# Handing five kinds of buffers to the most urgent tile, with a trace to plan and a trace to build

## The chip, the cores and the metric

The kernel runs on one NeuronCore of a Trainium2 chip. A core has five engines that run side by side, each in its own program order: TensorE (PE in the profile; its weight loads are shown apart as PEld), VectorE (DVE), ScalarE (ACT), GpSimd (POOL) and SyncE (SP), which here issues nearly all DMA transfers. Engines wait for each other through semaphores. The metric is the device time of one execution in microseconds (us), as the median over runs.

## The reference

One inference step of a small decoder of two layers, for a prompt of 2048 tokens and for 8 sample tokens that share the weights and have 2048 cached positions each. All arithmetic is float32. Cut to what matters:

```python
for layer in range(2):
    if layer == 0:   # even: gated MLP (A) beside stick-breaking attention (B)
        u, v, gate_a, q, k, vb, gate_b = split(x @ w_in_even)
        out_a = chunk_spatial_gate(gelu(u), standardize(gelu(v))) * silu(gate_a)
        z = q @ k.T * HEAD_DIM ** -0.5
        att = exp(log_sigmoid(z) + later)      # later: reversed cumulative sum of log_sigmoid(-z)
        out_b = (att @ vb) * silu(gate_b)
    else:            # odd: attention over 256 selected keys (C) beside causal pooling (D)
        q, kv, q_idx, k_idx, w_idx, gate_c, p, gate_d = split(x @ w_in_odd)
        index = einsum(relu(q_idx @ k_idx.T), w_idx)
        sel = top_k(index, 256)
        out_c = softmax(q @ k[sel].T + bias) @ v[sel] * silu(gate_c)
        out_d = (windowed_means(p) - p) @ w_grp * scale * silu(gate_d)
    x = layer_norm(alpha * x + concat(outs) @ w_out[layer])
```

The outputs are the two activations and the new cache rows of both layers.

## The kernel before

**The work.** The prompt goes in four blocks of 512 tokens. `load_xT` transposes a block of x, `p0` (layer 0) and `p1a`, `p1b` (layer 1) project it, `mixer_b` is the attention B, `select` and `topk` find the 256 keys, `c_tiles` is the attention C, `out_proj` the output projection, `ln_late` and `ln` the layer norm. The sample tokens go along in `sample0` and `sample1`. Projections are three float32r matmuls for each float32 one: high part by high part, low by high, high by low (`pp` at L735 to L737, `pp_o` at L1132 to L1134); ScalarE casts the high part of a weight (L661) and VectorE subtracts the low part (L664).

`run` weaves these generators into one traced program. In B, a tile `z` of logits comes from TensorE (L1027), ScalarE reads it out (L1031 or L1034), VectorE scans it (L1041), TensorE transposes the result (`ps_p`, L1064), ScalarE copies it back (L1065), and `av` sums it up (L1073). In C, `z_c` (L1763) is read out by VectorE together with its maximum (L1765), ScalarE takes the exponential (L1781), TensorE transposes (`ps_pc`, L1794), ScalarE copies back (L1796), and `av_c` sums (L1808). The indexer's scores are `z_i` (L1453), read by ScalarE (L1456). At the end of each `topk` VectorE runs a conditional (L1595) that goes into an exact search only if there are ties.

**The buffers.** A tile comes from a pool under a tag, and tiles of one tag share a number of buffers. In PSUM each of the tags `pp`, `pt` and `pz` has two buffers of one bank (2 KB a partition). `BANKS` says which tile uses which: `pp` takes pp, pp_o, ps_ki, ps_kv; `pz` takes z, z_c, z_i, ps_s, ps_m; `pt` takes ps_p, ps_pc, ps_x and every other name that is not listed. In SBUF the tags `tmp` and `ot` have four buffers each; `tmp` holds short-lived pieces, among them lng and lnb, the gains and offsets of the layer norm (L1210, L1211), and `ot` holds loaded pieces (xc, the transposed block's input, and ot, the input of `out_proj`).

**What sets the order.** After the trace the class `Order` replans it. `gather` collects the dependencies, the tiles' users (`uses`) and for each tag the tiles in traced order (`tags`). `plan` is a list scheduler: it steps through time with costs by `cost` (a conditional counts 400 ns) and picks on each engine the ready instruction of smallest `rank`; ranks come from `latest`, which runs the plan backwards. An instruction is ready when its predecessors are done and its tiles have buffers. `settle` makes plans for three guesses of the costs, with five rounds each, and keeps the one that `replay` finds shortest under two draws of the costs. `keep` hands each engine's order to the framework, which makes the semaphores and assigns buffers.

In `plan`, `take` hands out buffers: for each tag strictly in traced order, and only when the tile that got the last one has begun (`open_`):

```python
while queue[g] and free[g] and open_[g]:
    x = queue[g].pop()
    if gone[g]:
        self.after[x] = gone[g].pop(0)
    free[g] -= 1
    open_[g] = False
```

`after` notes which tile left the buffer that x gets.

Of the kernel before, what the change touches and what calls it, by code (L numbers as in the profile page):

```python
# [11 lines left out]
F32 = mybir.dt.float32  # L12
# [10 lines left out]
P = 128  # L23
# [59 lines left out]
}  # L83


class Order:


    ENGINES = {"PE": "PE", "DVE": "DVE", "Activation": "ACT", "Pool": "POOL", "SP": "SP"}
    SEM, DMA_START, DMA_END, RATE = 200, 700, 1500, 280.0  # L90
    TILED, STAY, PATIENT = 150, 500, 40e3
    GUESSES = ((1.0, 200), (1.0, 250), (1.04, 230))
    ROUNDS, DRAWS, SPREAD = 5, 2, 0.05
    TAIL = {"ACT": 100, "POOL": 45, "DVE": 75}
# [47 lines left out]
    def gather(self):  # L142
# [83 lines left out]
        for t in sorted(self.uses, key=lambda t: self.uses[t][0]):  # L226
            if self.tiles[t].space != DRAM:
                self.tags.setdefault(self.tiles[t].tag, []).append(t)


    def cost(self, n):
# [83 lines left out]
        return (i.opcode in ("TensorScalarPtr", "TensorCopy") and len(i.outs) == 1 and self.size(i.outs[0]) > 1  # L315
                and all(map(sb, (*full, i.outs[0]))))

    def settle(self):

        N, eng = len(self.ins), self.eng  # L320
        self.costs = [self.cost(n) for n in range(N)]
        for g, ms in self.group.items():
            busy = sum(self.costs[m][0] for m in ms)
            self.costs[g] = busy, busy + 170
        self.dma = [e is not None and "DMA" in i.opcode for e, i in zip(eng, self.ins)]
        self.kinds = [self.kind(n) for n in range(N)]
        self.ports = [self.port(n) for n in range(N)]
        self.succ = [[] for _ in range(N)]
        for n, d in enumerate(self.dep):
            for m in d:  # L330
                self.succ[m].append(n)
        self.links()
        draws, mid, best = [self.draw(k) for k in range(self.DRAWS)], self.costs, None
        sem = self.SEM
        for by, near in self.GUESSES:
            self.costs = [(b * by, l * by) if e in self.TAIL else (b, l) for e, (b, l) in zip(eng, mid)]
            self.SEM = near
            self.plan(list(range(N)))
            for _ in range(self.ROUNDS):
                self.SEM = near  # L340
                self.plan(self.latest())
                self.SEM = sem
                x = sum(self.replay(c) for c in draws)
                if best is None or x < best[0]:
                    best = x, self.order, self.after
        self.costs, (_, self.order, self.after) = mid, best

    def draw(self, seed):

# [75 lines left out]
    def turns(self):  # L425
# [11 lines left out]
            last[e] = n  # L437
        return out

    def plan(self, rank):  # L440

        N, eng, push, pop = len(self.ins), self.eng, heapq.heappush, heapq.heappop
# [2 lines left out]
        for g, ts in self.tags.items():  # L445
            for t in ts:
                home[t] = g
                for n in self.uses[t]:
                    left[n] += 1 + (n != self.uses[t][0])
                    tiles[n].append(t)  # L450
        queue = {g: ts[::-1] for g, ts in self.tags.items()}
        free = {g: max(self.tiles[t].tag_meta.bufs for t in ts) for g, ts in self.tags.items()}
        open_ = dict.fromkeys(queue, True)
        users = {t: len(u) for t, u in self.uses.items()}
        self.after, gone = {}, {g: [] for g in queue}
        since, done, self.begun = [0.0] * N, [0.0] * N, [0.0] * N
        ready, idle = {e: [] for e in self.ENGINES.values()}, dict.fromkeys(self.ENGINES.values(), 0.0)
        self.order = {e: [] for e in ready}
# [7 lines left out]
                push(due, (since[n], n))  # L466

        def take(g, t):
            while queue[g] and free[g] and open_[g]:
                x = queue[g].pop()  # L470
                if gone[g]:
                    self.after[x] = gone[g].pop(0)
                free[g] -= 1
                open_[g] = False
                for n in self.uses[x]:
                    release(n, t)

# [5 lines left out]
        while count < N:  # L483
            while back and back[0][0] <= now:
                _, g, x = pop(back)
                free[g] += 1
                gone[g].append(x)
                take(g, now)
            while due and due[0][0] <= now:
                n = pop(due)[1]  # L490
# [7 lines left out]
            for e, q in ready.items():  # L498
                while q and idle[e] <= now:
                    n, until = q[0][1], hold.get(self.OTHER.get(e), 0.0)  # L500
                    if e == "PE" and (kinds[n] == "h") != (kind == "h"):
                        same = [x for x in q if (kinds[x[1]] == "h") == (kind == "h") and x[0] <= q[0][0] + self.STAY]
                        if same:
                            n = min(same)[1]
                            q.remove(min(same))
                            heapq.heapify(q)
                            push(q, (-math.inf, n))
                    if e == "SP" and self.dma[n] and dma_end > now + self.DMA_START and last + rank[n] > now + self.PATIENT:
                        late.append(dma_end - self.DMA_START)
                        break  # L510
                    if ports[n] and until > now:
                        free_ = [x for x in q if not ports[x[1]] and now + cost[x[1]][0] <= until + self.SLACK]
                        if not free_:
                            late.append(until)
                            break
                        n = min(free_)
                        q.remove(n)
                        heapq.heapify(q)
                        n = n[1]
                    else:  # L520
                        pop(q)
                    s, (busy, lat) = now, cost[n]
                    if ports[n]:
                        hold[e] = s + max(40, busy - self.RELEASE[e])
                    if e == "PE" and now > idle[e] + 1 and kinds[n] == kind:
                        busy, lat = busy + self.RESTART, lat + self.RESTART
                    if e == "PE" and kinds[n] != kind:
                        s += self.TILED if "h" in (kinds[n], kind) else 0
                        kind = kinds[n]
                    self.begun[n] = s  # L530
                    if self.dma[n]:
                        dma_end = max(s + self.DMA_START, dma_end) + lat
                        done[n] = dma_end + self.DMA_END
                    else:
                        done[n] = s + lat
                    idle[e] = s + busy
                    self.order[e] += [*self.before.get(n, ()), *self.group.get(n, (n,))]
                    count += 1
                    moved = True
                    for m in succ[n]:  # L540
                        release(m, s + 1 if e == "PE" and eng[m] == "PE" else done[n] + self.SEM)
                    for t in tiles[n]:
                        g, u = home[t], self.uses[t]
                        if n == u[0]:
                            open_[g] = True
                            for m in u[1:]:
                                release(m, s)
                            take(g, s)
                        users[t] -= 1
                        if not users[t]:  # L550
                            push(back, (max(done[m] for m in u) + self.SEM, g, t))
# [59 lines left out]
                now = max([now] + [min(then)] if then else [now])  # L611
        return [-s - c[0] for s, c in zip(start, cost)]

    def keep(self):
        info = mybir.DependencyInfo(mybir.DependencyClass.NoSync, mybir.DependencyReason.DATA)
        for o in self.order.values():
            for a, b in zip(o, o[1:]):
# [5 lines left out]


class Body:
    def __init__(self, ctx, tc, I, O):
        self.ctx, self.tc, self.nc, self.I, self.O = ctx, tc, tc.nc, I, O
        pool = lambda n, b, **k: ctx.enter_context(tc.tile_pool(name=n, bufs=b, **k))
        self.cst = pool("cst", 1)
        self.sm = pool("sm", 4)  # L630
        self.dr = pool("dr", 1, space=DRAM)
        self.banks = {n: pool(n, 2, space=PSUM) for n in ("pp", "pt", "pz")}
        self.act = pool("act", 8)
        self.wp = pool("wp", 2)
        self.loc = pool("loc", 4)
        self.bufs = BUFS
# [30 lines left out]
    def rsqrt(self, out, var, eps, n):  # L667
# [9 lines left out]
        for _ in range(3):  # L677
# [2 lines left out]
            v.tensor_scalar(t[:n], t[:n], -0.5, 1.5, op0=OP.mult, op1=OP.add)  # L680
            v.tensor_tensor(out, out, t[:n], op=OP.mult)

    def ps(self, name, shape=(P, TB)):

        b = next(b for b in BANKS.get(name, "pt").split() if b in self.banks)
        return self.banks[b].tile(list(shape), F32, tag=b, name=name)

    def tmp(self, name):
        return self.loc.tile([P, TB], F32, tag="tmp", name=name, bufs=self.bufs["tmp"])

    def tok(self, name, n=TB):
        return self.loc.tile([P, TB + 16], F32, tag="tok", name=name, bufs=self.bufs["tok"])[:, :n]
# [392 lines left out]
            nc.sync.dma_start(self.otd[0][i][4 + m], sm)  # L1085

    def otile(self, name):
        return self.loc.tile([P, TB], F32, tag="ot", name=name, bufs=self.bufs["ot"])

    def out_parts(self, i, layer, last):  # L1090

# [1370 lines left out]
         ('new_d_buf_prompt', (1, 1, 15, 512)), ('new_d_buf_sample', (1, 8, 15, 512))]  # L2462


def build(nc, shapes):
    I = {n: nc.dram_tensor(n, s, d, kind="ExternalInput").ap() for n, s, d in shapes}
    O = {n: nc.dram_tensor("out_" + n, s, F32, kind="ExternalOutput").ap() for n, s in _OUTS}
    with tile.TileContext(nc, schedule_with_timeline_sim=True) as tc:
        with ExitStack() as ctx:
            body = Body(ctx, tc, I, O)  # L2470
            body.run()
        order = Order(tc, body.lags)
        order.gather()
        order.settle()
        order.keep()


# [11 lines left out]
```

## Time and profile before

| | |
|---|---|
| median of 3 runs | 2790.44 us (2785.44 to 2792.58) |
| the profiled execution | 2784.49 us |
| its span, first to last instruction | 2782.8 us |
| instructions | 52464 |
| HBM read and written | 431.33 MB and 89.73 MB, 187 GB/s over the span |

The page cuts the span into 40 slices; a digit is the busy share of a slice in tenths. TensorE's and VectorE's rows and the granted TensorE clock:

```profile
PE   9999999999999999989899999999999999899996
DVE  3466568775857886747988888897898788888865
PEclk9999999999999999999999999999999999999998
```

A busy TensorE is not one at its peak, because matmuls overlap and their ends are modelled. In the lists of waits each row says which instruction waited (engine, tile written, line), what came last before it could go, how many us in total, how often, and the longest.

### The profile page before, as it was taken

To read this page: it belongs to the slowest core of one execution; us is meant where nothing else is said; L and a number is where in the kernel's file an instruction comes from. 1 tells how busy PE (TensorE), PEld (TensorE's weight loads), DVE (VectorE), ACT (ScalarE), POOL (GpSimd) and SP (SyncE) were. 2 spreads that over 40 slices of the span, in tenths; PEclk is the share of its full clock that TensorE was granted. 3 is DMA by queue.
4 is the path that set the end of the run, shared out by engine and by line. 5 is a ranking of instruction groups with operands and counts; after the bars stand their busy time and mean duration, and the time that the engine had idled before them with its cause. 6 is when DMAs were issued, how large, how long until landed. Compare 5 with 4: busy or idle time off the path is not lost. (4 is left out here: it accounts for less than half of the span.)

```text
span 2782.8 us, 52464 instructions
## 1 busy us (share of the span) xinstructions
PE 2672.8 (96%) x17490; PEld 2154.5 (77%) x17490; DVE 2060.9 (74%) x5557; ACT 1604.3 (58%) x3216; POOL 766.3 (28%) x1040
## 2 busy tenths in 40 slices
PE   9999999999999999989899999999999999899996
PEld 7888787777777887768677677778777889898985
DVE  3466568775857886747988888897898788888865
ACT  3434333444444354435657677786686788688854
POOL 0111112210202321033433522334411445344222
PEclk9999999999999999999999999999999999999998
DMA  8666857895777777563764545433675666767462
GB/s 251 168 186 207 266 169 245 242 302 161 224 213 205 222 207 249 181 178 116 211 199 132 166 131 157 127 102 115 190 220 149 199 192 200 221 200 235 125 197 81
DMA packets 538914, 524.58 MB, mean 189 GB/s; under 512 B 43447, under 2 KB 411224, under 8 KB 538607
## 3 DMA queue, kind: packets, MB, share of 16 engines
q1 hardware_dynamic: 528759, 485.34, 58.9%
q0 software_dynamic: 9856, 35.66, 4.1%
q8 instruction: 139, 2.28, 0.3%
q14 instruction: 160, 1.31, 0.1%
HBM read 431.33 MB, written 89.73 MB: 187 GB/s over the span
## 5 line engine op out<-in xcount | busy, mean ns | idle before, releaser
L735 PE MATMUL pp<-xh,wh 128*128 128x512 f32 (+1 forms) x1536 | 624.0, 408 | 2.5 <-ACT wh L661 1.6
L736 PE MATMUL pp<-xl,wh 128*128 128x512 f32 (+1 forms) x1536 | 615.4, 401 | 0.0
L737 PE MATMUL pp<-xh,wl 128*128 128x512 f32 (+1 forms) x1536 | 613.6, 400 | 0.0
L664 DVE TENSOR_TENSOR wl<-wr,wh 128x512 fp32r<-128x512 f32 x520 | 354.5, 699 | 161.7 <-ACT wh L661 146.8
L661 ACT CAST wh<-wr 128x1024 fp32r<-128x1024 f32 x260 | 270.2, 1040 | 321.4 <-PE pp L736 160.2
L735 PEld LDWEIGHTS pp<-xh,wh 128*128 128x128 f32 (+1 forms) x1536 | 287.6, 188 | 67.4 <-issue 8.5
L737 PEld LDWEIGHTS pp<-xh,wl 128*128 128x128 f32 (+1 forms) x1536 | 287.6, 187 | 61.5 <-issue 4.4
L736 PEld LDWEIGHTS pp<-xl,wh 128*128 128x128 f32 (+1 forms) x1536 | 288.2, 188 | 53.9 <-issue 5.3
L1132 PE MATMUL pp_o<-wh,oh 128*128 128x256 f32 x1008 | 294.2, 294 | 5.4 <-DVE xres L1137 3.6
L1133 PE MATMUL pp_o<-wl,oh 128*128 128x256 f32 x1008 | 290.5, 289 | 0.2 <-DVE wl L664 0.2
L1134 PE MATMUL pp_o<-wh,ol 128*128 128x256 f32 x1008 | 288.5, 289 | 0.0
L1065 ACT COPY P<-ps_p 128x512 f32<-128x512 f32 (+2 forms) x320 | 166.5, 524 | 178.3 <-PE ps_p L1064 156.2
L1041 DVE TENSOR_TENSOR_SCAN P<-P,bfst 128x512 f32<-128x512 f32 x192 | 250.0, 1317 | 14.5 <-ACT P L1034 7.6
L1763 PE MATMUL z_c<-ksc,qc 128*128 128x512 f32 (+3 forms) x816 | 221.3, 356 | 22.9 <-DVE mx L1765 13.1
L1781 ACT ACTIVATE zt<-zt,nmax 128x512 f32<-128x512 f32 (+3 forms) x320 | 209.6, 657 | 54.1 <-DVE nmax L1769 52.2
L1750 POOL TENSOR_TENSOR nm<-nm,mk 128x256 f32<-128x256 f32 (+1 forms) x128 | 98.4, 770 | 420.2 <-DMA nm<-bft 161.3
L1796 ACT COPY zt<-ps_pc 128x512 f32<-128x512 f32 (+3 forms) x320 | 163.8, 522 | 81.6 <-PE ps_pc L1794 79.2
L1027 PE MATMUL z<-ks,q 128*128 128x512 f32 (+3 forms) x640 | 195.0, 390 | 13.1 <-DVE mx L1765 5.1
L1132 PEld LDWEIGHTS pp_o<-wh,oh 128*128 128x128 f32 x1008 | 193.3, 192 | 12.6 <-DVE xres L1137 4.6
L1133 PEld LDWEIGHTS pp_o<-wl,oh 128*128 128x128 f32 x1008 | 194.3, 193 | 4.1 <-issue 1.1
L1134 PEld LDWEIGHTS pp_o<-wh,ol 128*128 128x128 f32 x1008 | 193.4, 193 | 4.5 <-issue 2.2
L1509 ACT ACTIVATE mk<-ix,tk_tn 128x1152 int8<-128x1152 f32 (+13 forms) x140 | 183.8, 1313 | 17.7 <-DVE tk_tn L1559 6.6
(455 smaller groups left out, 5518.0 us busy)
## 6 DMA issues: line engine op xcount, KB each, us to landing
pg<-cache_b_kv SPq DMA_DIRECT2D x256, 256.0 KB
wr<-w_in_even SPq DMA_DIRECT2D x112, 512.0 KB
wr<-w_in_odd SPq DMA_DIRECT2D x76, 512.0 KB
wr<-w_out SPq DMA_DIRECT2D x68, 512.0 KB
ks<-ksc SPq DMA_DIRECT2D x80, 256.0 KB
ksc<-kcs SPq DMA_DIRECT2D x80, 256.0 KB
q<-qsc SPq DMA_DIRECT2D x64, 256.0 KB
qc<-qcs SPq DMA_DIRECT2D x128, 128.0 KB
```

The source lines that it names most:

```text
L661: nc.scalar.copy(hi, raw)
L664: e.tensor_tensor(lo[:, c], raw[:, c], hi[:, c].bitcast(F32), op=OP.subtract)
L735: nc.tensor.matmul(ps[:m], wh[:, kt, :m], xh[kt], start=a, stop=False)
L736: nc.tensor.matmul(ps[:m], wh[:, kt, :m], xl[kt], start=False, stop=False)
L737: nc.tensor.matmul(ps[:m], wl[:, kt, :m], xh[kt], start=False, stop=b)
L1027: nc.tensor.matmul(z[:, :n], q2[:, c, t * P:(t + 1) * P].bitcast(F32R), ks[:, :n].bitcast(F32R), start=c == 0, stop=c == 1)
L1041: nc.vector.tensor_tensor_scan(r, r, r, initial=ini, op0=OP.mult, op1=OP.bypass)
L1132: nc.tensor.matmul(ps[:, :256], oh[:, tt], wh[:, k], start=a, stop=False)
L1133: nc.tensor.matmul(ps[:, :256], oh[:, tt], wl[:, k], start=False, stop=False)
L1134: nc.tensor.matmul(ps[:, :256], ol[:, tt], wh[:, k], start=False, stop=b)
L1763: nc.tensor.matmul(z[:, :n], q2[:, c, jj % 2, :].bitcast(F32R), kk, start=c == 0, stop=c == 1)
L1781: nc.scalar.activation(zt, zt, AF.Exp, bias=nmx, accum_out=st["rs"][:, h, c:c + 1])
```

## The change

`plan` may now hand out the buffers of five tags (`FREELY`: ot, tmp, pt, pz, pp) in another order than the traced one. For these tags `choose` looks at the eight tiles of smallest rank (rank of a tile's first instruction) and takes the first that can have a free buffer. Each buffer must still see its tiles in traced order, so a tile may take a buffer only if the buffer's last holder stands earlier in the trace. `safe` goes through the remaining tiles in traced order and asks whether each finds a buffer whose holder's last use lies before its first use. `pending` is the tile that has a buffer but hasn't begun: while there is one, only a tile that stands earlier in the trace can get one too. `AHEAD`, a bound on how far a tile may be ahead, is a million and so does not bind.

`plan` now says which buffer each tile gets (`slot`), and the framework has to follow: the program is traced twice. The first trace ends in `keep` with the exception `Planned`, which carries the orders, `after`, and a list of slots for each tag. The second trace runs on a new program object; `turn` gives each tile of the five tags a tag of its own for its buffer (`pz0`, `pz1`, ...) with one buffer each, and `settle` takes the orders as they are. The computation is the same.

The diff, cut to its core:

```diff
+FREELY = ('ot', 'tmp', 'pt', 'pz', 'pp')
...
+    AHEAD, WINDOW = 10**6, 8
...
+        last = lambda n: max(self.group.get(n, (n,)))
+        self.span = {t: (u[0], max(map(last, u))) for t, u in self.uses.items()}
+        self.free = {g for g, ts in self.tags.items() if g.split("_")[0] in FREELY}
...
-    def settle(self):
+    def settle(self, plan):
...
+        if plan:
+            self.order, self.after = plan[:2]
+            return
...
+    def safe(self, queue, held, x, b):
+
+        held = [(f, self.span[t][1] if t else -1) for f, t in held]
+        if x:
+            held[b] = self.span[x]
+        far = max(f for f, _ in held)
+        for t in queue:
+            if t == x:
+                continue
+            first, end = self.span[t]
+            if first > far:
+                return True
+            fit = [(f, k) for k, (f, e) in enumerate(held) if f < first and e < first]
+            if not fit:
+                return False
+            held[max(fit)[1]] = first, end
+        return True
+
+    def choose(self, queue, urgent, free, held, pending, any_):
+
+        least = queue[0]
+        if pending and (not any_ or self.span[pending][0] < self.span[least][0]):
+            return None
+        for x in urgent[:self.WINDOW] if any_ and not pending else ():
+            first = self.span[x][0]
+            if x != least and first > self.span[least][0] + self.AHEAD:
+                continue
+            for _, b in sorted(((held[b][0], b) for b in free if held[b][0] < first), reverse=True):
+                if self.safe(queue, held, x, b):
+                    return x, b
+        fit = sorted(((held[b][0], b) for b in free if held[b][0] < self.span[least][0]), reverse=True)
+        for _, b in fit:
+            if self.safe(queue, held, least, b):
+                return least, b
+        return (least, fit[0][1]) if fit and not any_ else None
...
-            while queue[g] and free[g] and open_[g]:
-                x = queue[g].pop()
-                if gone[g]:
-                    self.after[x] = gone[g].pop(0)
-                free[g] -= 1
-                open_[g] = False
+            while queue[g] and free[g]:
+                x = self.choose(queue[g], urgent[g], free[g], held[g], open_[g], g in self.free)
+                if x is None:
+                    return
+                x, b = x
...
+                self.slot[x] = b
+                if held[g][b][1]:
+                    self.after[x] = held[g][b][1]
+                held[g][b] = self.span[x][0], x
+                open_[g] = x
...
-    def keep(self):
+    def keep(self, plan):
+        if not plan:
+            raise Planned(self.order, self.after, {g: [self.slot.get(t, 0) for t in ts] for g, ts in self.made.items()})
...
+    def turn(self, pool, shape, tag, name, **k):
+
+        if tag not in self.made:
+            return pool.tile(shape, F32, tag=tag, name=name, **k)
+        if self.slots:
+            k, tag = {"bufs": 1}, f"{tag}{self.slots[tag][len(self.made[tag])]}"
+        t = pool.tile(shape, F32, tag=tag, name=name, **k)
+        self.made[tag.rstrip("0123456789")].append(t.tensor.name)
+        return t
...
-    build(nc, [(n, a.shape, mybir.dt.from_np(a.dtype)) for n, a in arrays.items()])
+    shapes = [(n, a.shape, mybir.dt.from_np(a.dtype)) for n, a in arrays.items()]
+    try:
+        build(bacc.Bacc("TRN2", target_bir_lowering=False, num_devices=1), shapes)
+    except Planned as x:
+        build(nc, shapes, x.args)
```

`ps`, `tmp` and `otile` now get their tiles through `turn`.

More of the change, by code (lines that the diff above doesn't have):

```diff
@@ L83 @@
 }
+FREELY = ('ot', 'tmp', 'pt', 'pz', 'pp')
+class Planned(Exception):
+    pass
 class Order:
@@ L344, in settle @@
                 if best is None or x < best[0]:
-                    best = x, self.order, self.after
-        self.costs, (_, self.order, self.after) = mid, best
+                    best = x, self.order, self.after, self.slot
+        self.costs, (_, self.order, self.after, self.slot) = mid, best
     def draw(self, seed):
@@ L450, in plan @@
                     tiles[n].append(t)
-        queue = {g: ts[::-1] for g, ts in self.tags.items()}
-        free = {g: max(self.tiles[t].tag_meta.bufs for t in ts) for g, ts in self.tags.items()}
-        open_ = dict.fromkeys(queue, True)
+        queue = {g: list(ts) for g, ts in self.tags.items()}
+        urgent = {g: sorted(ts, key=lambda t: (rank[self.uses[t][0]], t)) if g in self.free else queue[g]
+                  for g, ts in self.tags.items()}
+        bufs = {g: max(self.tiles[t].tag_meta.bufs for t in ts) for g, ts in self.tags.items()}
+        free = {g: list(range(k)) for g, k in bufs.items()}
+        held = {g: [(-1, None)] * k for g, k in bufs.items()}
+        open_ = dict.fromkeys(queue)
         users = {t: len(u) for t, u in self.uses.items()}
-        self.after, gone = {}, {g: [] for g in queue}
+        self.after, self.slot = {}, {}
         since, done, self.begun = [0.0] * N, [0.0] * N, [0.0] * N
@@ L468, in take @@
         def take(g, t):
-            while queue[g] and free[g] and open_[g]:
-                x = queue[g].pop()
-                if gone[g]:
-                    self.after[x] = gone[g].pop(0)
-                free[g] -= 1
-                open_[g] = False
+            while queue[g] and free[g]:
[3 more added lines that the diff above has]
+                x, b = x
+                queue[g].remove(x)
+                if urgent[g] is not queue[g]:
+                    urgent[g].remove(x)
+                free[g].remove(b)
+                self.slot[x] = b
[3 more added lines that the diff above has]
+                open_[g] = x
                 for n in self.uses[x]:
@@ L485, in plan @@
                 _, g, x = pop(back)
-                free[g] += 1
-                gone[g].append(x)
+                free[g].append(self.slot[x])
                 take(g, now)
@@ L544, in plan @@
                         if n == u[0]:
-                            open_[g] = True
+                            open_[g] = None if open_[g] == t else open_[g]
                             for m in u[1:]:
@@ L625, with __init__ @@
 class Body:
-    def __init__(self, ctx, tc, I, O):
+    def __init__(self, ctx, tc, I, O, slots):
         self.ctx, self.tc, self.nc, self.I, self.O = ctx, tc, tc.nc, I, O
+        self.slots, self.made = slots, {g: [] for g in FREELY}
         pool = lambda n, b, **k: ctx.enter_context(tc.tile_pool(name=n, bufs=b, **k))
@@ L681, in rsqrt @@
             v.tensor_tensor(out, out, t[:n], op=OP.mult)
+    def turn(self, pool, shape, tag, name, **k):
[6 more added lines that the diff above has]
+        return t
     def ps(self, name, shape=(P, TB)):
         b = next(b for b in BANKS.get(name, "pt").split() if b in self.banks)
-        return self.banks[b].tile(list(shape), F32, tag=b, name=name)
+        return self.turn(self.banks[b], list(shape), b, name)
     def tmp(self, name):
-        return self.loc.tile([P, TB], F32, tag="tmp", name=name, bufs=self.bufs["tmp"])
+        return self.turn(self.loc, [P, TB], "tmp", name, bufs=self.bufs["tmp"])
     def tok(self, name, n=TB):
@@ L1087, in otile @@
     def otile(self, name):
-        return self.loc.tile([P, TB], F32, tag="ot", name=name, bufs=self.bufs["ot"])
+        return self.turn(self.loc, [P, TB], "ot", name, bufs=self.bufs["ot"])
     def out_parts(self, i, layer, last):
@@ L2462, with build @@
          ('new_d_buf_prompt', (1, 1, 15, 512)), ('new_d_buf_sample', (1, 8, 15, 512))]
-def build(nc, shapes):
+def build(nc, shapes, plan=None):
     I = {n: nc.dram_tensor(n, s, d, kind="ExternalInput").ap() for n, s, d in shapes}
@@ L2469, in build @@
         with ExitStack() as ctx:
-            body = Body(ctx, tc, I, O)
+            body = Body(ctx, tc, I, O, plan and plan[2])
             body.run()
@@ L2473, in build @@
         order.gather()
-        order.settle()
-        order.keep()
+        order.made = body.made
+        order.settle(plan)
+        order.keep(plan)
 def kernel(**inputs):
```

## Prediction

> **What bounds the kernel now.** I read the page's first part for the engine nearest to full, then the cores, then the span cut at the first and the last matmul, then what TensorE waited for, and last the timeline around the longest of those waits and at the end.
>
> ```profile
> span 2782.8 us, 52464 instructions
> PE 2672.8 (96%) x17490; PEld 2154.5 (77%) x17490; DVE 2060.9 (74%) x5557; ACT 1604.3 (58%) x3216; POOL 766.3 (28%) x1040
> ...
> L735 PE MATMUL pp<-xh,wh 128*128 128x512 f32 (+1 forms) x1536 | 624.0, 408 | 2.5 <-ACT wh L661 1.6
> ```
>
> ```profile
> core 0: 2782.8 us, clock 0.983
> ```
>
> ```profile
> 0.00:10.00 10.00, 4.04 (x18) 3.17 (x19) 5.77 (x34) 4.08 (x5) 1.03 (x12) 1.00 0.83 219
> 10.00:2757.80 2747.80, 2668.73 (x17474) 2151.38 (x17472) 2042.59 (x5491) 1597.19 (x3207) 755.90 (x1022) 0.99 0.63 189
> 2757.80:2782.80 25.00, 0.00 (x0) 0.00 (x0) 12.54 (x34) 3.04 (x4) 9.33 (x7) 0.59 0.52 169
> ```
>
> The span is 2782.8 us; this execution took 2784.5 us, 6 us under the median of the runs, 2790.44. The first number behind the comma is TensorE's busy time. In the long middle stretch it lacks 2747.80 - 2668.73 = 79 us; before it 6 us go to loading, after it there are 25 us without a matmul. So TensorE sets the pace and a reordering can win its 79 us of idle time, what of its clock was withheld, a part of the last 25 us, and no more of what is visible. The clock: 1 - 0.983 of 2782.8 us is 47 us of withheld clock, of which (1 - 0.59) x 25 = 10 us lie after the last matmul, where they cost nothing; 37 us lie in the middle.
>
> What TensorE waited for (us in total, times, longest):
>
> ```profile
> PE z_c L1763 <- DVE mx L1765: 13.1, 8, 3.6
> PE ps_so L2304 <- DMA s_pg<-cache_c_kv,s_rq: 7.0, 4, 2.4
> PE z_i L1453 <- DMA qi<-qis: 5.4, 2, 5.1
> PE z L1027 <- DVE mx L1765: 5.1, 1, 5.1
> PE ps_p L1064 <- ACT P L1065: 4.6, 4, 1.9
> PE z L1027 <- DMA ks<-ksc: 4.4, 3, 2.4
> ...
> PE pp_o L1132 <- DVE xres L1137: 3.6, 3, 2.1
> PE z_c L1763 <- ACT r L1456: 2.7, 4, 1.6
> PE z L1027 <- ACT P L1031: 2.2, 3, 1.4
> ...
> PE z_c L1763 <- DVE mx L1399: 2.0, 1, 2.0
> ...
> PE ps_kv L1332 <- ACT kv_tok L1334: 1.6, 1, 1.6
> ...
> PE ps_s L968 <- DVE sb L971: 1.5, 1, 1.5
> PE z_i L1453 <- ACT r L1456: 1.4, 4, 0.6
> ...
> PE pp_o L1132 <- ACT oh L648: 0.9, 1, 0.9
> ...
> PE ps_x L711 <- DMA xc<-x: 0.9, 2, 0.5
> ```
>
> The waits on an eviction by VectorE or ScalarE are waits for a buffer of `pz` (z, z_c, z_i, ps_s: 13.1 + 5.1 + 2.7 + 2.2 + 2.0 + 1.5 + 1.4 = 28.0), of `pt` (ps_p, 4.6) and of `pp` (pp_o, ps_kv: 5.2). Together 37.8 us of the 79. They are what the change can speak to: a tile stands at its bank because the two before it in the traced order were not yet read out, or a later one could have gone first.
>
> **The change, part by part.** *The choice of the tile.* Five tags hand a free buffer to the tile with the smallest rank among the next eight, if the tiles left over still fit. No instruction is added to the kernel or taken away; every engine's order is planned anew, with SP's queue of loads. Of the 37.8 us, not all can go, since the longest waits have a cause behind the buffer:
>
> ```profile
> 1557.80 1.01 DVE L1511 TENSOR_SCALAR_CACHE_REDUCE mk<-ix,tk_tn 128x768 int8<-128x768 f32 x1 [3.63 <-DVEq L1595]
> ...
> 1561.87 0.56 DVE L1765 CUSTOM_DVE_ANT_0 zt<-z_c,mk 128x384 f32<-128x384 f32 x1 [3.05 <-issue]
> ```
>
> ```profile
> 1562.49 1.01 PE L1027 MATMUL z<-ks,q 128*128 128x384 f32 x2 [5.11 <-DVE mx L1765]
> ```
>
> VectorE stood at the conditional of L1595 for 3.63 us and then 3.05 us more, and only then read z_c; TensorE waited 5.11 us. No naming of buffers shortens that; what it could do is put a projection or a `z` (read by ScalarE) in front. Ends for this term: 0 (each wait comes back elsewhere) and 37.8 (all go). I take the half, 19 us, because the rows are nearly half and half: 13.1 + 5.1 hang on the eviction at L1765 that such a conditional holds up, the other 19.6 on short evictions.
>
> *The clock.* Around the 5.1 us wait at 1250 us the granted clock (the number behind the five engines) was
>
> ```profile
> 1240.00:1258.00 18.00, 10.78 (x60) 9.02 (x58) 7.62 (x20) 4.84 (x11) 6.24 (x14) 0.69 0.78 207
> 1258.00:1275.00 17.00, 16.55 (x101) 14.19 (x102) 12.00 (x26) 11.79 (x27) 6.50 (x12) 0.82 0.40 117
> 1275.00:1320.00 45.00, 45.00 (x340) 37.51 (x341) 36.01 (x111) 21.38 (x51) 14.28 (x24) 1.00 0.41 120
> ```
>
> so idle stretches are followed by a lowered clock, here 0.82 in 17 us with TensorE 97% busy. If the middle's 37 us shrink as its idle time does, 19 of 79, that is 9 us; ends 0 and 37. The Trainium skill says the same of the cause (TensorE: Matmul & The Clock Gate, What's actually happening): the gate goes by windows of about 3.4 us and halves the clock after an idle one. By that rule alone only the three waits of 3.6, 5.1 and 5.1 us above reach a window; half a window of 1.7 us each makes 5 us, half of them 2.5, and the sum would come to 2774.5 us. The trace agrees that the dip stands right behind a long wait, but (1 - 0.82) x 17 = 3.1 us were lost behind this one alone.
>
> *The price.* A tile that overtakes takes its buffer out of the traced order, and until the trace has reached it, the tiles before it go through the other buffer, one by one. What such a tile costs:
>
> ```profile
> 1554.04 0.48 PE L1027 MATMUL z<-ks,q 128*128 128x256 f32 x2
> ```
>
> ```profile
> 1554.81 0.39 ACT L1031 ACTIVATE P<-z 128x256 f32<-128x256 f32 x1
> ```
>
> from the matmul's start to the end of ScalarE's read 1555.20 - 1554.04 = 1.16 us, of which 0.48 are TensorE's own: up to 0.7 us a tile when nothing else is ready. The nearest rows of such a wait are ps_p on ACT P and z on ACT P above, 6.8 us in 7, 1.0 us each. Ends: 0, if other matmuls stand in the gap (the usual case, with projections in flight), and some 30 us (30 new waits). I take 8 new ones, 8 us, since at most the shorter end is paid where projections run.
>
> *`ot` and `tmp`, and the end.* The SBUF tags feed loads: x and oh. TensorE lost 0.9 us each to them above; gain 0 to 2, taken as 0, for SP's own order hides it. At the end tmp's four buffers hold the gains and offsets of the layer norm, and the last rows' are asked for last:
>
> ```profile
> 2768.05 6.37 DMA lng<-ln_g
> ```
>
> ```profile
> 2772.91 1.26 POOL L1215 TENSOR_TENSOR xres<-xres,lng 128x512 f32<-128x512 f32 x1 [5.03 <-DMA lng<-ln_g]
> ```
>
> The last rows waited 5.03 us for a gain whose load could start only when the sample rows gave a buffer back. If the urgent tile goes first, up to 5 us are won; but then the sample rows come late by as much. Ends -5 and +5; I take 2 us of gain.
>
> *A first trace that ends in an exception, and tags of one buffer each in the second.* That is work at build time and costs the chip nothing. The waits between the tiles of one buffer are the same kind as before; those of the other slot fall away. Nothing is costed here; its cover is that the plan's orders are kept by the same edges.
>
> **The sum.** 19 + 9 + 2 - 8 = 22 us off the profiled 2784.5: 2762.5. The runs' median lay 6 us over this profile, so 2768 us is my number, 0.8% faster.
>
> **Rivals.**
>
> *The waits only move.* For it: the rows at L1595 and L1765. VectorE, 74% busy over all, is the late one there, and a tile that goes first lets another stand at the same eviction. The Trainium skill (PSUM — Partial Sum Buffer, Engine vs sequencer instructions) says VectorE's and ScalarE's queues are strictly in order and matmuls start in program order, so whatever is planned behind the branch stands still; the trace agrees at 1557.80. Against it: 19.6 us of the 37.8 aren't of that kind. It gives what is left of the sum with those 18.2 us and the clock kept and the price paid: 9.8 + 2 - 8 = 4 us, 2786 us. That the change does little because the rank rarely differs from the trace comes out here too.
>
> *One buffer too few (the slower side).* Overtaking leaves the tiles behind with a single bank, which for `pz` means that TensorE stands up to 0.7 us, and 1.0 us in the measured cases. It outweighs the gains of 30 us from some 30 such waits on. For it: TensorE has nowhere else to go where no projection runs, as around 1250 us; the planner costs a conditional at 400 ns where the row above shows 3.63 us, so its order doesn't hold on VectorE. Against it: the rows of one bank's tiles waiting now are short and few (4.6 in 4, 2.2 in 3). At 45 such waits, 19 + 9 + 2 - 45 = 15 us lost: 2805 us.
>
> *More than is visible.* Matmuls' ends overlap: L735's take 408 ns in the mean, yet start 0.23 us apart here:
>
> ```profile
> 1722.34 0.39 PE L735 MATMUL pp<-xh,wh 128*128 128x512 f32 x1
> 1722.57 0.39 PE L736 MATMUL pp<-xl,wh 128*128 128x512 f32 x1
> ```
>
> so a stall of up to 0.17 us each hides inside "busy". If the change smooths those as well, one 10 ns step on each of the 3 x 1536 projection matmuls is 46 us. With two thirds of the visible gain (15 us) that makes 61: about 2730 us. The Trainium skill (Perfetto Trace Analysis, its opening note) warns that matmul busy time is a bad metric for the same reason. Against it: the weight loads, 77% busy, leave little air in the projections, and nothing in the change shortens a switch between two kinds of matmul.
>
> **How the numbers follow.** The forecast (8 to 45 us won) gets 0.54, more than that 0.10, waits that only move 0.18, the lost bank 0.18. About 0.3%, 8.4 us, is what a measurement of this kernel tells from no change. Faster: 0.54 + 0.10 = 0.64; within: 0.18; slower: 0.18. The range for 8 in 10 goes from 2738 (most of the large case left out) to 2802 (a part of the slower one left out); the forecast's own range is 2745 to 2782.
>
> **What would show it.** Right: TensorE's idle time between first and last matmul falls from 79 to about 60 us, the z_c and z waits on the eviction at L1765 from 18.2 to under 12, the clock from 0.983 to about 0.986, the order of z, z_c and z_i in `pz` differs from before, instruction count equal to within the semaphores. Wrong: idle time stays near 79 with new rows of ps_p, z or pp_o waiting on their own evictions (one bank too few), or the idle time falls and TensorE's busy time rises by as much, from more changes between kinds of matmul; or the last lng's load still comes at the end with the same 5 us.

## The result and the profile after

| | before | after |
|---|---|---|
| median (range) of the runs | 2789.86 us (2785.44 to 2792.58, 4 runs) | 2755.03 us (2753.71 to 2756.58, 4 runs) |
| the profiled execution | 2784.49 us | 2756.58 us |
| its span | 2782.8 us | 2754.8 us |

The ratio of the times is 0.9877, with a 95% interval of 0.986 to 0.9894: 34.8 us, or 1.2%, faster. The two profiled executions lie 28 us apart, because the one of before is at the low end of its runs and the one of after is the slowest of its four; what follows is balanced against those 28 us.

The lines of the code moved by 64 to 74: the projections L735 are L809 now, `z` L1027 is L1101, the eviction L1765 is L1839, `z_i` L1453 is L1527, the casts L648 and L661 are L712 and L725.

The head of the page of after, and its clock:

```profile
span 2754.8 us, 52415 instructions
PE 2664.5 (97%) x17490; PEld 2151.0 (78%) x17490; DVE 2052.2 (74%) x5557; ACT 1599.5 (58%) x3216; POOL 774.0 (28%) x1040
```

```profile
core 0: 2754.8 us, clock 0.985
```

The number of matmuls, vector and scalar instructions is the same; the 49 fewer in all lie among those that the page doesn't count as busy. The span of after cut at the same two places (the columns as in the prediction: length, then busy time of TensorE, its weight loads, VectorE, ScalarE, GpSimd, then granted clock):

```profile
0.00:10.00 10.00, 4.24 (x18) 3.08 (x19) 5.60 (x33) 4.08 (x5) 1.03 (x12) 1.00 0.81 211
10.00:2729.90 2719.90, 2659.53 (x17470) 2147.38 (x17469) 2032.49 (x5490) 1592.35 (x3207) 763.01 (x1021) 0.99 0.64 191
2729.90:2754.80 24.90, 0.76 (x7) 0.55 (x5) 14.15 (x36) 3.10 (x5) 9.93 (x8) 0.57 0.49 170
```

The middle is 27.9 us shorter (2747.80 before, 2719.90 now). Its idle TensorE time is 2719.90 - 2659.53 = 60.4 us instead of 79.1, which is 18.7 us; the other 9.2 us are busy time (2668.73 to 2659.53) with the same matmuls in it. The withheld clock of the middle is (1 - 0.985) x 2754.8 - (1 - 0.57) x 24.9 = 31 us instead of 37. The loading at the start is as long as it was, and so is the end: 25.0 us before, and 24.9 us now, in which 0.76 us of matmuls still run.

What TensorE waited for in after:

```profile
PE z_c L1837 <- DVE mx L1839: 15.6, 14, 2.9
PE pp_o L1206 <- ACT oh L712: 4.9, 2, 3.5
...
PE z_i L1527 <- DVE mx L1839: 4.0, 3, 2.4
PE ps_so L2378 <- DMA s_pg<-cache_c_kv,s_rq: 3.6, 4, 1.5
PE pp_o L1206 <- DVE xres L1211: 2.8, 4, 1.2
...
PE z L1101 <- DMA ks<-ksc: 2.6, 3, 1.2
PE ps_x L785 <- DMA xc<-x: 2.6, 3, 1.6
...
PE z L1101 <- ACT P L1105: 1.5, 1, 1.5
...
PE z L1101 <- DVE mx L1839: 1.0, 1, 1.0
...
PE ps_p L1138 <- ACT P L1139: 0.5, 1, 0.5
```

`z_c` and `z` still wait for the late eviction, now at L1839: 15.6 + 1.0 = 16.6 us, where before had 18.2; only the single waits are shorter (2.9 us at most, before 5.1). `z_i` now waits 4.0 us there, where it waited 0.9. The rows of short evictions did shrink (`ps_p` on ScalarE 4.6 to 0.5 us, `z` on ScalarE 2.2 to 1.5, `pp_o` on VectorE 3.6 to 2.8). Waits for loads shrank as well: the 5.4 us of `z_i` on `qi` are gone, `ps_so` went from 7.0 to 3.6, `z` on `ks` from 4.4 to 2.6. Against that, `pp_o` waits 4.9 us for the cast `oh` and `ps_x` 2.6 us for its load `xc`.

Then I asked where in the span the time went. The 613th and the 817th matmul at `ps_p` bound nearly the same work in each kernel (1748 and 1741 matmuls here): the join, in which layer 0 ends, its layer norm runs and layer 1 begins. For before and for after:

```profile
1181.46:1500.08 318.62, 295.23 (x1748) 230.19 (x1744) 235.48 (x653) 175.58 (x377) 113.99 (x164) 0.97 0.60 170
```

```profile
1180.21:1483.38 303.17, 289.28 (x1741) 225.96 (x1740) 233.75 (x656) 173.43 (x375) 115.88 (x164) 0.99 0.63 178
```

Here alone 15.4 of the 28 us are won: 9.5 us idle (318.62 - 295.23 = 23.4, against 13.9) and 5.9 us busy, at a clock of 0.99 instead of 0.97. After is 1.3 us ahead where the join begins and 16.7 us where it ends; the other 11.3 us are won behind it, spread out: from each 68th matmul at `ps_p` to the next no step there is over 6 us.

In the join there is a place that shows what a buffer of `tmp` can hold up. `kw` is the piece into which ScalarE reads a finished projection. TensorE in before, around it:

```profile
1365.39 0.63 PE L737 MATMUL pp<-xh,wl 128*128 128x512 f32 x2
...
1383.71 0.49 PE L735 MATMUL pp<-xh,wh 128*128 128x512 f32 x1
```

For 18 us no projection runs. The `pp` bank of `kw` is full, and its read-out waits, since `lng` and `lnb` of the layer norm were traced earlier and hold `tmp`'s buffers. GpSimd is done with `lng` only here:

```profile
1381.42 1.26 POOL L1215 TENSOR_TENSOR xs_ln<-xs_ln,lng 8x512 f32<-8x512 f32 x1
```

```profile
1382.71 0.58 ACT L1291 COPY kw<-pp 36x512 f32<-36x512 f32 x1 [0.46 <-POOL xs_ln L1215]
```

The copy starts right as GpSimd ends. `pp`'s other bank doesn't help, though it was read out by 1368: the next tile of `pp` in traced order is `ps_ki`, which transposes `kw` (L1301) and so can't begin before this copy either. The projections resume right behind it:

```profile
1383.35 0.43 PE L1301 MATMUL ps_ki<-idf,kw 36*128 36x36 f32 x4 [0.32 <-ACT kw L1291]
```

The copy stands in no list as a long wait, because ScalarE did other work meanwhile and was idle for 0.46 us only. In after `kw` goes past `lng` and is read 1.9 us after the last matmul of its tile starts, at 1352.92:

```profile
1352.92 0.39 PE L811 MATMUL pp<-xh,wl 128*36 128x512 f32 x1
```

```profile
1354.84 0.58 ACT L1365 COPY kw<-pp 36x512 f32<-36x512 f32 x1
```

### The profile page after: what moved, and what is told of

The parts are those of the page before. It is cut to its first block, busy times and chain, and to the rows that moved or that the text cites. A ratio compares the mean times of both kernels' runs of the same rounds, so it can differ in the third digit from the quotient of the medians.

```text
span 2754.8 us, 52415 instructions
## 1 busy us (share of the span) xinstructions
PE 2664.5 (97%) x17490; PEld 2151.0 (78%) x17490; DVE 2052.2 (74%) x5557; ACT 1599.5 (58%) x3216; POOL 774.0 (28%) x1040
## 5 line engine op out<-in xcount | busy, mean ns | idle before, releaser
L809 PE MATMUL pp<-xh,wh 128*128 128x512 f32 (+1 forms) x1536 | 624.3, 408 | 3.4 <-ACT wh L725 1.9
L725 ACT CAST wh<-wr 128x1024 fp32r<-128x1024 f32 x260 | 270.0, 1040 | 309.5 <-PE pp L810 132.5
L809 PEld LDWEIGHTS pp<-xh,wh 128*128 128x128 f32 (+1 forms) x1536 | 287.4, 187 | 68.2 <-issue 7.9
L1837 PE MATMUL z_c<-ksc,qc 128*128 128x512 f32 (+3 forms) x816 | 223.2, 359 | 19.9 <-DVE mx L1839 15.6
L1101 PE MATMUL z<-ks,q 128*128 128x512 f32 (+3 forms) x640 | 191.1, 383 | 6.3 <-DMA ks<-ksc 2.6
L1583 ACT ACTIVATE mk<-ix,tk_tn 128x512 int8<-128x512 f32 (+13 forms) x140 | 183.6, 1311 | 23.0 <-DVE tk_tn L1633 11.8
```

The source lines that it names most:

```text
L725: nc.scalar.copy(hi, raw)
L809: nc.tensor.matmul(ps[:m], wh[:, kt, :m], xh[kt], start=a, stop=False)
L1101: nc.tensor.matmul(z[:, :n], q2[:, c, t * P:(t + 1) * P].bitcast(F32R), ks[:, :n].bitcast(F32R), start=c == 0, stop=c == 1)
L1837: nc.tensor.matmul(z[:, :n], q2[:, c, jj % 2, :].bitcast(F32R), kk, start=c == 0, stop=c == 1)
```

## The experiments

Two theories at the start. The banks: overtaking in `pp`, `pt` and `pz` wins, as the prediction had it. The pieces in SBUF: overtaking in `tmp` (and `ot`) wins, since a piece of the layer norm no longer holds up a read-out. The rivals beside them are that naming the buffers does it, or that it is the luck of a new plan.

Each run was timed beside executions of the kernel before, whose medians were 2785.4, 2780.4 and 2780.3 us in three groups of runs, and not 2790. So the ratios count; a gain in us is the ratio's, taken of 2790 us, and the expected times are to be read against 2790 too. A join is that of one execution.

**Naming the buffers alone.** Two traces, a tag for each buffer, but all tiles in traced order:

```diff
-        self.free = {g for g, ts in self.tags.items() if g.split("_")[0] in FREELY}
+        self.free = {g for g, ts in self.tags.items() if g.split("_")[0] in ()}
```

> Two traces and one tag for each buffer as in the changed kernel, but the planner hands every tag out in traced order. Theory A (the freedom to overtake wins the time): as before the change, 2790 us, within 8. Theory N (what wins is that the framework must follow the planner's own buffers): as after the change, 2755 us.

Ratio to before 0.999 (0.997 to 1.0011). Naming wins nothing.

**The banks alone.**

```diff
-        self.free = {g for g, ts in self.tags.items() if g.split("_")[0] in FREELY}
+        self.free = {g for g, ts in self.tags.items() if g.split("_")[0] in ("pt", "pz", "pp")}
```

> Only pt, pz and pp may overtake; ot and tmp go in traced order. Theory P (the prediction's: TensorE's waits at its banks are what goes): most of the 35 us, 2757 to 2767 us. Theory S (the SBUF pieces, whose loads and layer norms feed the start of a stage, win it): 2780 us or more.

Ratio 0.9974 (0.9956 to 0.9991), 7 us. The join:

```profile
1181.22:1493.73 312.51, 295.39 (x1745) 229.33 (x1742) 235.89 (x654) 174.24 (x377) 114.59 (x164) 0.98 0.61 173
```

The banks carry a small part of the 35 us: 2.5 to 12 us by the interval.

**The SBUF tags alone.**

```diff
-        self.free = {g for g, ts in self.tags.items() if g.split("_")[0] in FREELY}
+        self.free = {g for g, ts in self.tags.items() if g.split("_")[0] in ("ot", "tmp")}
```

> Only ot and tmp may overtake; the banks go in traced order. Theory P: hardly any gain, 2780 to 2792 us. Theory S: most of it, 2757 to 2770 us. If both halves win their part, this and the run with the banks alone add up to the 35 us.

Ratio 0.991 (0.9877 to 0.9944), 25 us. The join is as short as in after:

```profile
1178.66:1482.34 303.68, 290.02 (x1740) 227.50 (x1739) 228.85 (x646) 173.60 (x375) 115.38 (x163) 0.98 0.62 177
```

**The luck of a plan.** Before, with the guesses of the costs moved a little, so that the same rule gives another plan:

```diff
-    GUESSES = ((1.0, 200), (1.0, 250), (1.04, 230))
+    GUESSES = ((1.0, 210), (1.0, 240), (1.03, 220))
```

> The kernel before with the planner's three guesses changed a little (1.0, 210; 1.0, 240; 1.03, 220): another plan of the same freedom. It tells how much a plan's luck is worth. If a theory of the buffers holds, it stays within 8 us of 2790; if plans differ by chance by as much as the change won, it moves by 15 us or more.

Ratio 1.0026 (1.0012 to 1.0041). This one other plan differs by some 0.3%, so the 0.26% of the banks can't be told from luck. The 0.9% of the SBUF tags is more than that; but a later pair of plans differs by 0.7%, so no single run settles it, and the table below does.

**`tmp` alone, and `ot` alone.**

```diff
+        self.free = {g for g, ts in self.tags.items() if g.split("_")[0] in ("tmp",)}
```

> Only tmp may overtake. Theory S1 (at the join of the first and the second stage the projection's read-out kw must wait for a tmp buffer that the layer norm's gains hold): more than half of the 25 us that ot and tmp won together, 2768 to 2776 us. Theory S2 (the loads through ot, xc and the output projection's input, are what must come earlier): 2780 us or more.

```diff
+        self.free = {g for g, ts in self.tags.items() if g.split("_")[0] in ("ot",)}
```

> Only ot may overtake. Theory S1: within 8 us of before, 2780 to 2793 us. Theory S2: 2760 to 2775 us.

`tmp` alone: 0.9944 (0.9923 to 0.9965), with a join of

```profile
1180.91:1487.39 306.48, 291.67 (x1749) 228.22 (x1746) 239.47 (x665) 174.73 (x379) 119.07 (x166) 0.98 0.62 178
```

`ot` alone: 1.0026 (1.0014 to 1.0037). `ot` by itself wins nothing; `tmp` does. Whether `ot` adds anything to `tmp` isn't shown: 0.9944 and 0.991 with both have intervals that overlap.

**Overtaking only in the join, and only outside it.** Both with `ot` and `tmp` free. The numbers are places in the trace; a tile may overtake only if its first use lies between them, or only if it doesn't:

```diff
-            if x != least and first > self.span[least][0] + self.AHEAD:
+            if x != least and not 12400 <= first < 14200:
```

> ot and tmp may overtake, but a tile may be preferred to an earlier one only if its first instruction stands between 12400 and 14200 in the trace of 27492: the join of the first and the second stage, where the profile after is 18 to 20 us ahead of the one before by 1405 us. Theory J (the join wins it): 2764 to 2775 us. Theory E (many small gains everywhere): 2782 us or more.

```diff
-            if x != least and first > self.span[least][0] + self.AHEAD:
+            if x != least and 12400 <= first < 14200:
```

> The complement: ot and tmp may overtake everywhere but at that join. Theory J: 2778 us or more. Theory E: 2760 to 2770 us, nearly as with the freedom everywhere.

In the join only: 1.0007 (0.9997 to 1.0017). Outside only: 0.9937 (0.9921 to 0.9954). Their joins, in this order:

```profile
1176.96:1489.55 312.59, 293.57 (x1746) 229.62 (x1743) 229.80 (x646) 174.93 (x377) 111.55 (x163) 0.97 0.59 171
```

```profile
1176.59:1482.96 306.37, 292.31 (x1740) 227.71 (x1739) 230.35 (x651) 173.46 (x375) 112.23 (x163) 0.98 0.61 175
```

Theory J fell with both; the second run comes near theory E (0.9937 x 2790 = 2772 us). The two struck my reading of `kw` as well. From the start of its last matmul `kw` waits 13.8 to 27.5 us at this place in the six kernels of the table below that keep `tmp` in traced order, and 0.8 to 1.9 us in those that free it everywhere. With overtaking in the join only, it is read after 0.6 us, and nothing is won; with overtaking outside only, it waits 12.6 us, and 0.6% is won all the same, with a join 12 us shorter than before. So the wait of `kw` is real and the change cures it, but curing it isn't what wins the time, or not more than the luck of a plan can hide; overtakings traced before or behind the join shorten the join too.

**The first scores of layer 1.** The next candidate: in after, the tile `sb` (layer 0's read-out of `ps_s`, L971 in before) goes past `sg`, the last `ps_s` matmul comes 10 us earlier (1217.5 instead of 1227.7 us), and the indexer's `z_i` begins 12 us earlier, as I supposed because layer 0's pools come free. All `z_i` of before, and of after (count, shortest, median and longest ns, first and last start):

```profile
L1453 PE MATMUL z_i<-kid,qi x160: 220/398/668, 1234.5 to 2528.0; 128*128 128x512 f32 x112, 128*128 128x128 f32 x16, 128*128 128x256 f32 x16, 128*128 128x384 f32 x16
```

```profile
L1527 PE MATMUL z_i<-kid,qi x160: 220/396/668, 1222.4 to 2497.7; 128*128 128x512 f32 x112, 128*128 128x128 f32 x16, 128*128 128x256 f32 x16, 128*128 128x384 f32 x16
```

Two runs from both sides: the change with `sb` forbidden to overtake, and before with `sb` traced ahead of `sg`.

```diff
-            if x != least and first > self.span[least][0] + self.AHEAD:
+            if x != least and x.startswith("sb_"):
```

> The changed kernel, but a tile named sb may not be preferred to an earlier one. Theory R (sb, which reads ps_s, overtakes sg, so the last ps_s matmul and with it the pools of the first stage end some 10 us before the last projection, and the indexer's first z_i starts under the projections): z_i comes 7 to 12 us later again and the gain shrinks to a ratio of 0.990 to 0.993 to before. Rival T (the end of the first stage is made up later, and the gain is the sum of small ones): 0.986 to 0.9895, as after the change.

```diff
-            ps = yield from pj(8 + m)
-            sg = self.tmp("sg")
-            self.silu0(ps, sg)
-            nc.gpsimd.tensor_tensor(g, g, sg, op=OP.mult)
...
+            ps = yield from pj(8 + m)
+            sg = self.tmp("sg")
+            self.silu0(ps, sg)
+            nc.gpsimd.tensor_tensor(g, g, sg, op=OP.mult)
```

(The four lines move from ahead of the `ps_s` matmuls to behind `sb`.)

> The kernel before, buffers in traced order, but in p0 the matmuls ps_s and the tile sb are traced ahead of the gate's projection (8 + m) and its sg. No freedom, one tag's order changed by hand. Theory R: z_i starts 5 to 12 us earlier against the last projection, 0.995 to 0.9975 of before. Rival T: 0.9985 to 1.002.

With `sb` held back: 0.9902 (0.9882 to 0.9921). This time alone doesn't decide, as it lies in theory R's range and its interval reaches into T's. But `z_i` is as late as in before, and most of the gain is kept, with a join shorter than in any other run:

```profile
L1527 PE MATMUL z_i<-kid,qi x160: 220/396/775, 1234.1 to 2487.8; 128*128 128x512 f32 x112, 128*128 128x128 f32 x16, 128*128 128x256 f32 x16, 128*128 128x384 f32 x16
```

```profile
1182.33:1480.61 298.28, 289.69 (x1740) 225.44 (x1739) 233.84 (x649) 172.40 (x375) 119.42 (x163) 0.99 0.64 179
```

With `sb` traced first: 1.0023 (1.001 to 1.0036). The last `ps_s` matmul starts at 1218.7 us, the first `z_i` at 1229.2, 5.3 us earlier than before, and nothing is won. So an early `z_i` is neither needed for the short join nor enough for a gain.

**A sixth tag.** The change with `tok` (pieces in SBUF into which projections are read out) given out freely too:

```diff
-FREELY = ('ot', 'tmp', 'pt', 'pz', 'pp')
+FREELY = ('ot', 'tmp', 'pt', 'pz', 'pp', 'tok')
...
-        return self.loc.tile([P, TB + 16], F32, tag="tok", name=name, bufs=self.bufs["tok"])[:, :n]
+        return self.turn(self.loc, [P, TB + 16], "tok", name, bufs=self.bufs["tok"])[:, :n]
```

> The changed kernel with a sixth tag, tok (the projections' read-out pieces in SBUF), handed out by rank as well. If SBUF pieces that wait behind others' buffers are what the change cures, a little more is won: 0.983 to 0.987 of before. If only the banks or the one join count: 0.987 to 0.989.

Ratio 0.9888 (0.9867 to 0.9909): the same as the change. More freedom of this kind won nothing further, though the interval just reaches the range expected if it did.

**The luck of the change's own plan.** The change with the guesses moved as above:

```diff
-    GUESSES = ((1.0, 200), (1.0, 250), (1.04, 230))
+    GUESSES = ((1.0, 210), (1.0, 240), (1.03, 220))
```

> The changed kernel with the planner's guesses changed as in the run other_guesses: another plan of the same freedom. Its distance from the change is the luck of a plan: 0.985 to 0.991 if the freedom wins the time, over 0.995 if this one plan did.

Ratio 0.9944 (0.9926 to 0.9962). This lies between the two expectations: of the change's 1.2%, up to 0.7% hang on which plan it happened to get.

**All of it in one table**, by whether `tmp` keeps the traced order; the join is the stretch between the same two matmuls:

| kernel | `tmp` | banks | ratio to before | join, us |
|---|---|---|---|---|
| before | traced | traced | 1 | 318.6 |
| naming alone | traced | traced | 0.999 | 315.0 |
| other guesses, before | traced | traced | 1.0026 | 318.4 |
| `sb` traced first | traced | traced | 1.0023 | 318.2 |
| `ot` free | traced | traced | 1.0026 | 324.7 |
| banks free | traced | free | 0.9974 | 312.5 |
| free in the join only | in part | traced | 1.0007 | 312.6 |
| free outside the join only | in part | traced | 0.9937 | 306.4 |
| `tmp` free | free | traced | 0.9944 | 306.5 |
| `ot` and `tmp` free | free | traced | 0.991 | 303.7 |
| `sb` held back | free but `sb` | free | 0.9902 | 298.3 |
| other guesses, after | free | free | 0.9944 | 301.7 |
| `tok` too | free | free | 0.9888 | 308.8 |
| after | free | free | 0.9877 | 303.2 |

The six kernels with `tmp` wholly in traced order lie at 0.9974 to 1.0026, the seven in which it may overtake all along or outside the join at 0.9877 to 0.9944. They don't overlap, and no kernel of the first kind has a join under 312 us or of the second over 309. TensorE's idle time in the profiled executions (span less busy time) parts them likewise: 102 to 111 us in the six, 85 to 99 in the seven. That freedom in `tmp` is what most of the gain needs is shown. The means give sizes: five kernels with everything traced or only `ot` free 1.0013, the three with `tmp` and without banks 0.993, the four with both 0.9903. So some 0.8% (23 us) for `tmp` and 0.3% (8 us) for the banks; the second is no larger than what two plans of one rule differ by, so it is an estimate and not shown. The sizes are means of a few plans, of which two of one rule differed by up to 0.7%.

## Why the prediction was right, and where it wasn't

I said 2768 us and faster; it is 2755, 13 us below, inside the forecast's own range of 2745 to 2782. Two visible signs came as named: idle time from 79 to 60.4 us (60 was said), the clock to 0.985 (0.986). The reason given for them was mostly wrong.

- *The banks, 19 us.* The idle time that went is 18.7 us, but most of it isn't the term's. The banks alone give 7 us (the interval reaches from 2.5 to 12), and their profiled execution has 8 us less idle time than before; and the sign named for them failed: `z_c` and `z` behind the eviction should have come under 12 us and are at 16.6. Here the rival "the waits only move" was right: at that eviction `z_c`, `z` and `z_i` together wait 20.6 us, where they waited 19.1. With the clock that belongs to it and the price, the sum had 20 us here.
- *`ot` and `tmp`, 0 us.* This is the step that failed. `tmp` alone gives 0.0056 x 2790 = 16 us (10 to 21), with `ot` 25 us. I priced the tags by the waits of TensorE on their loads, 0.9 us each. But `tmp` holds no loads only: `kw`, `sb` and `sg` are read-outs of PSUM, and one behind `lng` keeps its bank and with it the projections. Nor did I look at the stretch where the layer norm and the next layer's projections run together, where half of the idle time that went had been (9.5 of 18.7 us). For `ot`, 0 was right.
- *The clock, 9 us.* Between the two profiled executions it measured 6 us, of 9.2 us of busy time that went from the middle. That it follows the idle time is not shown: the 25 executions of before timed beside the first experiments had clocks from 0.977 to 0.984 by themselves, and the kernel with overtaking in the join only has the idle time of before at a clock of 0.986 (last section). That one wait is followed by a lower clock does stand in the trace. In before, TensorE waits 2.05 us, and for the next 3.4 us, busy throughout, it gets half the clock (below). This agrees with the rule of the Trainium skill that an idle window halves the clock (TensorE: Matmul & The Clock Gate, What's actually happening). It differs from the prediction's reading of it, that only waits of about 3.4 us count: 2.05 us were enough here.

```profile
1495.87 0.58 PE L1763 MATMUL z_c<-ksc,qc 128*128 128x256 f32 x2 [2.05 <-DVE mx L1765]
```

```profile
1496.20:1499.60 3.40, 3.40 (x10) 2.60 (x9) 3.39 (x9) 1.18 (x3) 1.88 (x3) 0.50 1.06 269
```

- *The price, 8 us, and the rival "one buffer too few".* Hardly seen. The waits on a tile's own short eviction fell (`ps_p` 4.6 to 0.5 us), and the run with the banks alone wasn't slower than before.
- *The end, 2 us.* It measured about 1 us. As I had allowed, the last gain is still loaded at the end, and the last rows wait 5.18 us for it, where they waited 5.03:

```profile
2739.71 5.71 DMA lng<-ln_g
```

```profile
2745.57 2.48 POOL L1289 TENSOR_TENSOR xres<-xres,lng 128x512 f32<-128x512 f32 x2 [5.18 <-DMA lng<-ln_g]
```

- *"More than is visible".* TensorE's busy time fell by 8.3 us over the span, not by the 46 us of that rival, and the 6 us of clock explain most of it. L735's matmuls take 408 ns in the mean in both kernels (L809 in after), so nothing was smoothed there.

So two errors met. The banks with their clock and price came to 19 + 9 - 8 = 20 us in the sum and measured 7 alone; `tmp`, `ot` and the end came to 2 us and measured 25. The two measured parts make 32 of the 35 us. That the forecast came within 13 us is luck: the two errors have opposite signs, and the idle time that matched came from another tag than the one it was said of.

What stays open: which overtakings of `tmp` win. It isn't the one of `kw` by itself, nor that of `sb`, nor those traced in the join by themselves; those outside it are enough for 0.6%. A single place may not exist, since every edit makes a new plan of 52,000 instructions.

## What to carry to other kernels

Where one tag of scratch buffers serves both slow pieces (gains of a layer norm) and read-outs of PSUM, handing them out in traced order lets the slow ones hold a bank: look at the time from a tile's last matmul to its read-out, because such a wait stands in no list of idle time while the reading engine has other work (here 17 us, listed as 0.46). Curing one such wait need not win time, as `kw` shows. Price a buffer tag by everything it holds, not by its loads, and by the stretch where two stages overlap. Before a gain of under 1% in a planned kernel is put down to an edit, plan both kernels again with slightly moved costs: here that alone was 0.3% before and 0.7% after the change.

## What the hardware showed that I had not expected

TensorE's busy time for the same 17490 matmuls isn't a constant; in these runs it moves with the granted clock. Of the fourteen kernels, before with other guesses has the longest busy time and the change with `tok` the shortest:

```profile
die 0 (median of its cores): 2792.8 us, clock 0.981
...
PE 2681.9 (96%) x17490; PEld 2161.6 (77%) x17490; DVE 2053.6 (74%) x5557; ACT 1606.0 (58%) x3216; POOL 765.6 (27%) x1040
```

```profile
die 0 (median of its cores): 2753.2 us, clock 0.987
...
PE 2658.5 (97%) x17490; PEld 2148.6 (78%) x17490; DVE 2046.5 (74%) x5557; ACT 1599.3 (58%) x3216; POOL 778.7 (28%) x1040
```

The clock differs by 0.6% and the busy time by 23.4 us, 0.9%. It is tempting to say that idle time that goes takes busy time with it, since in the change 9.2 us went with 18.7. The kernel with overtaking in the join only speaks against that:

```profile
span 2773.7 us, 52436 instructions
PE 2664.8 (96%) x17490; PEld 2149.1 (77%) x17490; DVE 2051.9 (74%) x5557; ACT 1602.0 (58%) x3216; POOL 765.8 (28%) x1040
```

```profile
core 0: 2773.7 us, clock 0.986
```

Its idle time is 2773.7 - 2664.8 = 108.9 us, as in before (2782.8 - 2672.8 = 110.0), while its busy time is 8 us shorter, as short as in after. So the busy time went with the clock, and the clock of a single execution doesn't follow from its total of idle time.
